# Raw weights and cached keys through four half-size buffers, and two more steps ahead of the sample gate product, in a one-core streaming encoder step

## The chip, the cores and the metric

The kernel runs on one core of a Trainium2 chip. The metric is device time in microseconds (us), the median of several runs; less is better. A profile is one more execution, recorded instruction by instruction. The engines are PE (matrix multiply), DVE (vector), ACT (scalar, activations and copies), POOL (GpSimd) and SP, which here does nothing but issue transfers (DMAs) one after the other.

## The reference, cut to what matters

One layer of an encoder runs on 1024 prompt rows and on 8 sample streams of 16 new rows with 1024 cached rows each. Three mixers share one input projection: a stick-breaking attention group (`sb`), a forgetting-attention group (`fox`) and a state-space group (`ssd`). Cross-attention and a feed-forward block follow.

```
proj = u @ w_in                                # w_in: 1024 x 3084
sq, sk, sv, fq, fk, fv, fg, z, xbc, dt = split_last(proj, IN_SIZES)
sb_o  = sb_attend(sq, [past sb_k, sk], [past sb_v, sv])
fcum  = cumsum([past fox_logf, log_sigmoid(fg + b)])      # gate sums over 1024 + 16 rows
fox_o = softmax(q.k/8 + fcum[q] - fcum[k]) @ v
ssd_o = rmsnorm(ssd_scan(conv(xbc), dt, ...) * silu(z))
h = h + [sb_o, fox_o, ssd_o] @ w_out ; h = h + cross_attend(h) ; h = h + swiglu(h)
```

The weights and the cached keys are float32. A dense product is made of three matmuls: each factor is split into a rounded high part and the remainder, and high*high, high*low and low*high are added up.

## The kernel before, in words

**Weights.** `raw_t` hands out a raw buffer `wr` of 128 x 1056 floats; there are two. `w_unit` loads a piece of a weight (512 KB: eight row blocks of 128 columns, four of 256 or two of 512) into one `wr` with one transfer (L306), and `split_unit` makes the high part `wh` of it by one ACT copy of 1024 columns (L289) and the low part `wl` by four POOL subtractions of 256 columns (L132). The matmuls are in `mm3` (L314, L315, L316). In the projection of the memory the raw weights go through other tiles (`st`).

**Cached keys.** A decode step handles two streams (p = 0 to 3, for `sb` and for `fox`). `load_k` fetches 512 keys of a stream into one `wr` (L850, 512 KB), PE transposes them (L856, eight 128 x 128 blocks), ACT copies them to `kf` (L857, twice 512 columns), and PE multiplies the queries with them (L844). A step makes four such loads: two halves of the rows for two streams. They take their `wr` from the same two buffers as the weights do.

**Gate sums.** `fox_sums` scans the log gates. For the sample streams it loads the cached gates (L669, 16-byte pieces), transposes them (L678), adds the new ones (L685), scans 32 rows of 1040 on DVE (L687), stores the result (L688), and forms `fnew` by a small matmul, the sample gate product: DVE forms its factor (L692), PE multiplies it with `hsel` (L696), DVE copies the product (L697).

**Order.** Generators give the order in which the work is written down. `pipeline` runs the attention rows (`prompt_rows` L547 to L550, decode rows) and the products with the values (L565 transposes, L580; for decode L887, L896) of `sb` and then `fox`: 72 row steps and 40 value steps, 112 in all. After each of its steps one step of `fill_all` is taken, and 1.1 steps per step once the dense part is over. The dense part, `fill_s`, has 66 steps: four projections of three, the values with nine, `fox_sums` with two, `z` with nine and nine, `dt` with one, and eight conv blocks of three. Behind it comes `ssd_gen` with 51 steps (L1017 prepare, L1032 weights, L1057 and L1063 states, L1117 outputs, L1129 write). What is left of it when the pipeline ends is woven into the output projection, `heads_out`, two of its steps per `ssd` step. By this count 50 of the 51 are done when the pipeline ends. A scheduler then sets the final order on each engine from this program, dependences and priorities, so that neighbours in the program may end up apart. Each engine runs its list strictly in order, and SP issues its transfers strictly in order too.

**Norm ahead of the feed-forward block.** `scaled` squares a row block of h on ACT (L1741, 1024 columns, into a `wr` that nobody reads) and takes the row sum from the accumulator.

Of the kernel before, what the change touches and what calls it, by code (L numbers as in the profile page):

```python
# [17 lines left out]
P = 128  # L18
D = 1024
# [38 lines left out]
def f32(x):  # L58
    return x.bitcast(F32)
# [3 lines left out]
def tile_hybrid_step(ctx: ExitStack, tc: tile.TileContext, a: dict):  # L63
    nc = tc.nc
    ACT, DVE, POOL, PE, SP = nc.scalar, nc.vector, nc.gpsimd, nc.tensor, nc.sync
# [13 lines left out]
    ring = over.enter_context(tc.tile_pool(name="ring", bufs=3, side="right"))  # L79
# [206 lines left out]
    def split_unit(raw, n, eng=POOL, pair=None):  # L286
        hi, lo = pair or (ring.tile([P, 1056], F32R, tag="wh", name="wh"),
                          ring.tile([P, 1056], F32R, tag="wl", name="wl"))
        ACT.copy(hi[:, :n], raw[:, :n])  # L289
        if eng is POOL:  # L290
            pool_tt(lo[:, :n], raw[:, :n], f32(hi[:, :n]), ALU.subtract)
        else:
            eng.tensor_tensor(out=lo[:, :n], in0=raw[:, :n], in1=f32(hi[:, :n]), op=ALU.subtract)
# [305 lines left out]
    def sg2_t(dt=F32):  # L599
        return ptp.tile([P, 256], dt, tag="so", name="so", bufs=4)  # L600
# [45 lines left out]
    def fox_sums():  # L646
# [7 lines left out]
        for hf in range(2):  # L654
            tp = pd()
# [5 lines left out]
        tp = pd()  # L661
        for b in range(8):
# [7 lines left out]
                     in_=a["cache_fox_logf"][0].rearrange("b k h -> (b k) h").rearrange("(u p) h -> p u h", p=P))  # L670
# [4 lines left out]
        for hf in range(2):  # L675
            tp = pd()
# [15 lines left out]
        DVE.tensor_tensor(out=y8[0:32, :P].rearrange("p (b t) -> p b t", t=DEC_S),  # L692
                          in0=sr[:, PAST:].unsqueeze(1).to_broadcast([32, 8, DEC_S]),
# [117 lines left out]
    def decode_units(m):  # L811
# [15 lines left out]
        def rows(p):  # L827
# [17 lines left out]
                                                moving(g // 2, g % 2), start=True, stop=True) for g in (3, 0, 1, 2)])  # L845

            def load_k(hf, b2):
                raw = raw_t()
                rv = raw[:, :1024].rearrange("p (k c) -> p k c", c=256)
                SP.dma_start(out=rv, in_=ck[2 * p + b2, hf * 512:(hf + 1) * 512, :]  # L850
                             .rearrange("(k p) c -> p k c", p=P))
                kf = ring.tile([P, 1056], F32, tag=("wh", "wl")[b2], name="kf")
                for nb in range(2):
                    tp = pT()
                    for k in range(4):
                        PE.transpose(tp[:, k * P:(k + 1) * P], rv[:, k, nb * P:(nb + 1) * P], ident)  # L856
                    ACT.copy(kf[:, nb * 512:(nb + 1) * 512], tp)  # L857
                return kf

            def emit_past(hf):  # L860
# [696 lines left out]
    q = []  # L1557
# [175 lines left out]
    def scaled(blk):  # L1733

        if blk in (1, 3, 5, 7, 8):
            xs = h[(blk - 1) // 2 * 2:blk + 1] if blk < 8 else h[8:]
            b0, n = blk + 1 - len(xs), len(xs)
            ss, scratch = small(n), raw_t()
            for i, x in enumerate(xs):
                SP.dma_start(out=h_sc[(b0 + i) * P:(b0 + i + 1) * P, :], in_=x)  # L1740
                ACT.activation(scratch[:, :D], x, AF.Square, accum_out=ss[:, i:i + 1])  # L1741
            r = rstd_of(ss, n, 1.0 / D)
            yield
            for i, x in enumerate(xs):
                DVE.tensor_scalar(x, x, r[:, i:i + 1], None, ALU.mult)
            yield
        if blk in (1, 3):
            for kps in ((0, 1), (2, 3)):
                u = transposed(blk - 1, 2, kps)
                yield  # L1750
                yield from right_factors(0, blk - 1, 2, kps, u)
        if blk == 5:
            for _ in range(4):
                ahead.append(next(now))
                yield
# [181 lines left out]
```

## Time and profile before

| | |
|---|---|
| Median of the runs | 1937.82 us (1937.67, 1937.82, 1940.25) |
| The profiled execution | 1935.64 us |
| Its span, from the first to the last instruction | 1933.8 us |
| PE busy / DVE / ACT / POOL | 1843.4 / 898.4 / 816.6 / 628.4 us |
| Mean granted clock of PE | 0.983 |

The profiled execution lies 1.84 us above its span and 2.2 us below the median of the runs. "Busy" is the time in which an engine's instructions run; behind an engine's idle time the profile puts what ended it ("<-DMA wr<-cache_sb_k" is a transfer into `wr`). The granted clock is the share of its full clock at which PE was allowed to run.

### The profile page before, as it was taken

What the parts mean: (1) busy time and instruction counts of PE and PEld (TensorE: products, weight loads), DVE (VectorE), ACT (ScalarE), POOL (GpSimd) and SP (SyncE); (2) the same over time, 40 slices, a digit from 0 to 9 for tenths busy, and PEclk for the clock granted to TensorE, in tenths of its full rate; (3) what the DMA queues carried; (4) which work ended last, traced back from release to release, by engine and by line L of the source; (5) the groups of instructions that cost most, each with busy time, mean ns of one, the idle gap of its engine ahead of it and who ended that gap; (6) DMA issues with size and microseconds to landing.
All of it is one profiled execution on the core that took longest, in us unless ns stands there. A gap on an engine that the chain in (4) does not pass through costs nothing.

```text
span 1933.8 us, 32139 instructions
## 1 busy us (share of the span) xinstructions
PE 1843.4 (95%) x12128; PEld 1646.3 (85%) x12128; DVE 898.4 (46%) x1802; ACT 816.6 (42%) x1702; POOL 628.4 (32%) x918
## 2 busy tenths in 40 slices
PE   7989997999898899999999999999999999999997
PEld 5889776898876677889998888999999999888886
DVE  3421324466646783354445378333333333455554
ACT  6431543444656772143333165333333333344443
POOL 6632415263424563211101213554544443000000
PEclk9999997999999989999999999999999999999999
DMA  9455646455487878435559123322233223557572
GB/s 335 139 163 152 205 124 171 131 147 163 139 256 244 259 236 299 153 124 164 164 166 342 59 95 97 95 69 69 72 78 89 71 69 90 193 195 237 176 241 90
DMA packets 328923, 307.52 MB, mean 159 GB/s; under 512 B 88637, under 2 KB 292517, under 8 KB 328769
## 3 DMA queue, kind: packets, MB, share of 16 engines
q1 hardware_dynamic: 328768, 305.48, 51.5%
q8 instruction: 95, 1.56, 0.3%
q14 instruction: 60, 0.48, 0.1%
HBM read 229.31 MB, written 76.11 MB: 158 GB/s over the span
## 4 chain that ended last, share of the span: by engine, by line
PE 79%; DMA 6%; DVE 4%; ACT 2%; POOL 1%; issue 1%; SPq 0%; ACTq 0%; POOLq 0%; DVEq 0%
PE psd L1804 11%; PE psd L314 9%; PE psd L316 9%; PE psd L315 9%; PE pst L1804 8%; PE pss L1804 4%; PE pss L314 3%; PE pss L315 3%; PE pss L316 3%; PE pso L1804 2%; PE pso L580 2%; PE pst L314 1%; PE pst L315 1%; PE pst L316 1%; PE pst L565 1%
## 5 line engine op out<-in xcount | busy, mean ns | idle before, releaser
L132 POOL TENSOR_TENSOR wl<-wr,wh 128x256 fp32r<-128x256 f32 (+1 forms) x180 | 134.2, 778 | 241.2 <-ACT wh L289 208.9
L314 PE MATMUL psd<-act,wh 128*128 128x384 f32 x576 | 198.5, 345 | 5.2 <-DVE sg L441 2.6
L316 PE MATMUL psd<-act,wl 128*128 128x384 f32 x576 | 197.5, 343 | 0.1
L315 PE MATMUL psd<-act,wh 128*128 128x384 f32 x576 | 197.2, 342 | 0.0
L1804 PE MATMUL pst<-bT,tr 128*128 128x256 f32 (+1 forms) x1068 | 155.0, 293 | 0.0
L1804 PEld LDWEIGHTS pst<-bT,tr 128*128 128x128 f32 x1068 | 144.9, 188 | 0.1
L314 PE MATMUL psd<-wh,act 128*128 128x256 f32 (+3 forms) x414 | 134.2, 327 | 3.9 <-DMA act<-osc 1.1
L316 PE MATMUL psd<-wh,act 128*128 128x512 f32 (+3 forms) x424 | 136.9, 324 | 0.0
L315 PE MATMUL psd<-wl,act 128*128 128x256 f32 (+3 forms) x414 | 133.6, 324 | 0.5 <-POOL wl L132 0.5
L1804 PE MATMUL psd<-bT,tr 128*128 128x320 f32 (+1 forms) x912 | 133.2, 295 | 1.0 <-DVE tr L1651 0.5
L251 POOL TENSOR_SCALAR sm<-sm 128x1 f32<-128x1 f32 (+2 forms) x30 | 9.2, 307 | 377.6 <-ACT y L1899 291.8
L1804 PEld LDWEIGHTS psd<-bT,tr 128*128 128x128 f32 x912 | 124.7, 188 | 1.9 <-DVE tr L1651 0.7
L314 PEld LDWEIGHTS psd<-act,wh 128*128 128x128 f32 x576 | 109.3, 190 | 9.3 <-DVE sg L441 3.4
L132 POOL TENSOR_TENSOR tr<-u,tr 128x256 fp32r<-128x256 f32 x110 | 82.9, 782 | 99.2 <-ACT tr L1647 81.7
L132 POOL TENSOR_TENSOR ws<-ws 128x256 f32<-128x256 f32 (+2 forms) x100 | 78.5, 813 | 112.2 <-DVE ws L507 84.5
L316 PEld LDWEIGHTS psd<-act,wl 128*128 128x128 f32 x576 | 109.1, 189 | 2.0 <-issue 1.3
L315 PEld LDWEIGHTS psd<-act,wh 128*128 128x128 f32 x576 | 109.3, 190 | 0.8 <-issue 0.6
L1779 DVE TENSOR_TENSOR tr<-tr,pst 128x256 f32<-128x256 f32 (+1 forms) x86 | 38.6, 449 | 137.5 <-ACT tr L1776 104.4
L132 POOL TENSOR_TENSOR tr<-raw,tr 128x256 fp32r<-128x256 f32 x94 | 69.4, 768 | 86.2 <-ACT tr L1647 77.8
L289 ACT CAST wh<-wr 128x1024 fp32r<-128x1024 f32 (+2 forms) x45 | 47.0, 1050 | 106.2 <-PE psd L316 42.6
L314 PEld LDWEIGHTS psd<-wh,act 128*128 128x128 f32 x414 | 79.5, 192 | 11.9 <-issue 1.7
L1647 ACT CAST tr<-tr 128x384 fp32r<-128x384 f32 (+1 forms) x70 | 37.7, 538 | 122.0 <-DMA tr<-hidsc 112.8
(597 smaller groups left out, 4709.1 us busy)
## 6 DMA issues: line engine op xcount, KB each, us to landing
u<-w_down SPq DMA_DIRECT2D x40, 512.0 KB
raw<-w_down SPq DMA_DIRECT2D x26, 512.0 KB
st<-qksc SPq DMA_DIRECT2D x48, 256.0 KB
wr<-w_in SPq DMA_DIRECT2D x22, 512.0 KB
tr<-hidsc SPq DMA_DIRECT2D x57, 192.0 KB
hidsc<-tr SPq DMA_DIRECT2D x34, 288.0 KB
qksc<-sg SPq DMA_DIRECT2D x48, 192.0 KB
wr<-cache_sb_k SPq DMA_DIRECT2D x16, 512.0 KB
```

The costliest lines, as they stand in the source:

```text
L132: POOL.tensor_tensor(out=out[:, a0:a1], in0=in0[:, a0:a1], in1=in1[:, a0:a1], op=op)
L251: POOL.tensor_scalar(v, ss, inv, EPS, ALU.mult, ALU.add)
L289: ACT.copy(hi[:, :n], raw[:, :n])
L314: PE.matmul(out, ah, bh, start=start, stop=False)
L315: PE.matmul(out, ah, bl, start=False, stop=False)
L316: PE.matmul(out, al, bh, start=False, stop=stop)
L565: PE.transpose(tp[:, o:o + P], w[:, (2 * kp + j) * P:(2 * kp + j + 1) * P], ident)
L580: return PE.matmul(po[r:r + 64, q_], vt[:, 2 * (k0 + i) + j, :], pfs[i][:, sl], start=start and k0 == 0 and (j == 0 or qp > 0), stop=k0 + ...
L1647: ACT.copy(hi, src)
L1779: DVE.tensor_tensor(out=at(out, g), in0=at(x, g), in1=ps[g][:, :GW[g]], op=op)
L1804: PE.matmul(dst[g][:, :GW[g]], x[:, ka], y[:, k, :], start=start and k == 0 and m == 0, stop=stop and k == 3 and m == 2, skip_group_check= ...
```

## The change

The two raw buffers become four of 528 columns. `w_unit` loads a piece as two halves with a transfer each (twice as many transfers, half the size, the same bytes and rows) and rounds each half by itself (two ACT copies of 512 columns in place of one of 1024; POOL's subtractions stay 256 wide). `load_k` loads 512 keys as two halves of 256 and transposes and copies half by half: 4 + 4 blocks, and each of its two ACT copies now writes two runs of 256 columns. The projection of the memory, which brings its own raw tiles, is as before. `scaled` squares two halves of 512 into two buffers, with an accumulator read each and one DVE addition (128 x 1 or 128 x 2). `fox_sums` gets two empty steps between the store of the scan and the sample gate product, so the dense part has 68 steps; by the count above 48 of the 51 `ssd` steps are then done when the pipeline ends, and three are woven into `heads_out`.

```diff
     def raw_t():
-        return ring.tile([P, 1056], F32, tag="wr", name="wr", bufs=2)
+        return ring.tile([P, 528], F32, tag="wr", name="wr", bufs=4)
...
     def w_unit(srcs, k0, nk, raw=None, pair=None, eng=POOL):
         n = sum(s[2] for s in srcs)
-        raw = raw_t() if raw is None else raw
-        rv = raw[:, :nk * n].rearrange("p (k n) -> p k n", n=n)
-        o = 0
-        for w, c0, cn in srcs:
-            SP.dma_start(out=rv[:, :, o:o + cn],
-                         in_=w[k0 * P:(k0 + nk) * P, c0:c0 + cn].rearrange("(k p) n -> p k n", p=P))
-            o += cn
-        hi, lo = split_unit(raw, nk * n, eng, pair)
+        raws = [raw_t(), raw_t()] if raw is None else [raw]
+        nk_ = nk // len(raws)
+        for i, r in enumerate(raws):
+            rv = r[:, :nk_ * n].rearrange("p (k n) -> p k n", n=n)
+            o = 0
+            for w, c0, cn in srcs:
+                r0 = (k0 + i * nk_) * P
+                SP.dma_start(out=rv[:, :, o:o + cn],
+                             in_=w[r0:r0 + nk_ * P, c0:c0 + cn].rearrange("(k p) n -> p k n", p=P))
+                o += cn
+        hi, lo = pair or unit_pair()
+        for i, r in enumerate(raws):
+            sl = slice(i * nk_ * n, (i + 1) * nk_ * n)
+            split_into(hi[:, sl], lo[:, sl], r[:, :nk_ * n], eng)
...
         for p in range(4):
             SP.dma_start(out=fqs[:, p:p + 1], in_=fs_sc[8 * p:8 * p + 8, 0, PAST:PAST + DEC_S])
+        yield
+        yield
         y8 = sg2_t()
...
             def load_k(hf, b2):
-                raw = raw_t()
-                rv = raw[:, :1024].rearrange("p (k c) -> p k c", c=256)
-                SP.dma_start(out=rv, in_=ck[2 * p + b2, hf * 512:(hf + 1) * 512, :]
-                             .rearrange("(k p) c -> p k c", p=P))
+                rvs = []
+                for q in range(2):
+                    rvs.append(raw_t()[:, :512].rearrange("p (k c) -> p k c", c=256))
+                    k0 = hf * 512 + q * 256
+                    SP.dma_start(out=rvs[q], in_=ck[2 * p + b2, k0:k0 + 256, :].rearrange("(k p) c -> p k c", p=P))
                 kf = ring.tile([P, 1056], F32, tag=("wh", "wl")[b2], name="kf")
-                for nb in range(2):
+                for q in range(2):
                     tp = pT()
-                    for k in range(4):
-                        PE.transpose(tp[:, k * P:(k + 1) * P], rv[:, k, nb * P:(nb + 1) * P], ident)
-                    ACT.copy(kf[:, nb * 512:(nb + 1) * 512], tp)
+                    for nb in range(2):
+                        for k in range(2):
+                            PE.transpose(tp[:, (2 * nb + k) * P:(2 * nb + k + 1) * P], rvs[q][:, k, nb * P:(nb + 1) * P],
+                                         ident)
+                    ACT.copy(kf[:, :1024].rearrange("p (n c) -> p n c", n=2)[:, :, q * 256:(q + 1) * 256],
+                             tp.rearrange("p (n c) -> p n c", n=2))
...
-            ss, scratch = small(n), raw_t()
+            ss, s2 = small(n), small(2 * n)
             for i, x in enumerate(xs):
                 SP.dma_start(out=h_sc[(b0 + i) * P:(b0 + i + 1) * P, :], in_=x)
-                ACT.activation(scratch[:, :D], x, AF.Square, accum_out=ss[:, i:i + 1])
+                for j in range(2):
+                    ACT.activation(raw_t()[:, :512], x[:, j * 512:(j + 1) * 512], AF.Square,
+                                   accum_out=s2[:, j * n + i:j * n + i + 1])
+            DVE.tensor_tensor(out=ss, in0=s2[:, 0:n], in1=s2[:, n:2 * n], op=ALU.add)
```

The scheduler's order changes with it on every engine, up to the cross-attention; behind that it is nearly the same. Three places matter below. In these rows the names are those of the tiles (`pss`, `psd`, `pst`, `pso` are banks of the result memory), and the changed file's line numbers are 12 to 18 higher at these lines.

The first is PE around the sample gate product (the row with `hsel`). Before:

```order
L685 MATMUL psd<-fold,so 32x16
L547 MATMUL pss<-st 128x128
L548 MATMUL pss<-st 128x128
L550 MATMUL pss<-mask_sb,identr 128x128
L547 MATMUL pss<-st 128x256
L548 MATMUL pss<-st 128x256
L550 MATMUL pss<-mask_sb,identr 128x128
L547 MATMUL pss<-st 128x384
L548 MATMUL pss<-st 128x384
L550 MATMUL pss<-mask_sb,identr 128x128
L696 MATMUL psd<-so,hsel 128x128
L756 MATMUL psd<-ident,xc 128x24 x8
```

And now, from the same small product (`fold`) on:

```order
L697 MATMUL psd<-fold,so 32x16
L559 MATMUL pss<-st 128x128
L560 MATMUL pss<-st 128x128
L562 MATMUL pss<-mask_sb,identr 128x128
L559 MATMUL pss<-st 128x256
L560 MATMUL pss<-st 128x256
L562 MATMUL pss<-mask_sb,identr 128x128
L559 MATMUL pss<-st 128x384
L560 MATMUL pss<-st 128x384
L562 MATMUL pss<-mask_sb,identr 128x128
L710 MATMUL psd<-so,hsel 128x128
L770 MATMUL psd<-ident,xc 128x24 x8
```

The same nine attention matmuls stand between the two products: the two empty steps moved nothing here, and one attention row more now follows behind the product.

The second is SP, where the cached gates for that scan are loaded (`cache_fox_logf`), with the last two key loads of a decode step ahead of it. Before:

```order
L475 DMA vsc_196<-so 128x256
L850 DMA wr<-cache_sb_k 128x4x256 x2
L669 DMA sg<-cache_fox_logf 128x64x4
L596 DMA mixsc<-sg 64x2x256
L306 DMA wr<-w_in 128x4x256
```

Now:

```order
L487 DMA vsc_196<-so 128x256
L866 DMA wr<-cache_sb_k 128x2x256 x3
L608 DMA mixsc<-sg 64x2x256
L866 DMA wr<-cache_sb_k 128x2x256
L681 DMA sg<-cache_fox_logf 128x64x4
L315 DMA wr<-w_in 128x2x256
```

The gate load has two transfers more ahead of it on the same queue, and a store (`mixsc`) that stood behind it.

The third is PE where the first `fox` rows meet the conv projection (the `mask_fx` rows). Before, a row's two pieces and the next row's first piece follow each other with only transposes between them:

```order
L731 MATMUL psd<-ident,so 27x128
L547 MATMUL pss<-st 128x512
L548 MATMUL pss<-st 128x512
L919 MATMUL pst<-fold_157,so 128x64
L565 MATMUL pst<-ident,ws 128x128 x8
L547 MATMUL pss<-st 128x128
L548 MATMUL pss<-st 128x128
L550 MATMUL pss<-mask_fx,identr 128x128
L547 MATMUL pss<-st 128x512
L548 MATMUL pss<-st 128x512
```

Now, from the conv block's tail transpose (`so`) at that place on:

```order
L745 MATMUL psd<-ident,so 27x128
L577 MATMUL pst<-ident,ws 128x128 x2
L562 MATMUL pss<-mask_fx,identr 128x128
L559 MATMUL pss<-st 128x512
L560 MATMUL pss<-st 128x512
L562 MATMUL pss<-mask_fx,identr 128x128
L577 MATMUL pst<-ident,ws 128x128 x3
L592 MATMUL pso<-pt,st 64x256 x4
L577 MATMUL pst<-ident,ws 128x128 x3
L326 MATMUL psd<-act,wh 128x384
```

Only one row of a single piece stands here now; the row ahead of it was begun 38 dense matmuls earlier, and the rows with two pieces come later, with dense matmuls between them.

More of the change, by code (lines that the diff above doesn't have):

```diff
@@ L284, in act_pair, with unit_pair, split_into, split_unit @@
                 lo[:, :KT * width].rearrange("p (k w) -> p k w", w=width))
[L286 to L289, printed above, removed]
+    def unit_pair():
+        return [ring.tile([P, 1056], F32R, tag=t, name=t) for t in ("wh", "wl")]
+    def split_into(hi, lo, raw, eng=POOL):
+        ACT.copy(hi, raw)
         if eng is POOL:
-            pool_tt(lo[:, :n], raw[:, :n], f32(hi[:, :n]), ALU.subtract)
+            pool_tt(lo, raw, f32(hi), ALU.subtract)
         else:
-            eng.tensor_tensor(out=lo[:, :n], in0=raw[:, :n], in1=f32(hi[:, :n]), op=ALU.subtract)
+            eng.tensor_tensor(out=lo, in0=raw, in1=f32(hi), op=ALU.subtract)
+    def split_unit(raw, n):
+        hi, lo = unit_pair()
+        split_into(hi[:, :n], lo[:, :n], raw[:, :n])
         return hi, lo
     def raw_t():
-        return ring.tile([P, 1056], F32, tag="wr", name="wr", bufs=2)
+        return ring.tile([P, 528], F32, tag="wr", name="wr", bufs=4)
     def w_unit(srcs, k0, nk, raw=None, pair=None, eng=POOL):
         n = sum(s[2] for s in srcs)
-        raw = raw_t() if raw is None else raw
-        rv = raw[:, :nk * n].rearrange("p (k n) -> p k n", n=n)
-        o = 0
-        for w, c0, cn in srcs:
-            SP.dma_start(out=rv[:, :, o:o + cn],
-                         in_=w[k0 * P:(k0 + nk) * P, c0:c0 + cn].rearrange("(k p) n -> p k n", p=P))
-            o += cn
-        hi, lo = split_unit(raw, nk * n, eng, pair)
+        raws = [raw_t(), raw_t()] if raw is None else [raw]
[12 more added lines that the diff above has]
+            split_into(hi[:, sl], lo[:, sl], r[:, :nk_ * n], eng)
         return (hi[:, :nk * n].rearrange("p (k n) -> p k n", n=n),
```

## The prediction

> **What bounds the kernel now.** I read the page first, then the busy time in stretches of 40 us, then what PE waited for, then the timeline at the longest waits.
>
> The page's span and its row of engines:
>
> ```profile
> span 1933.8 us, 32139 instructions
> PE 1843.4 (95%) x12128; PEld 1646.3 (85%) x12128; DVE 898.4 (46%) x1802; ACT 816.6 (42%) x1702; POOL 628.4 (32%) x918
> ```
>
> PE is the bound: it is idle for 90.4 us of 1933.8, and no other engine reaches half. So the change can win only a part of those 90 us, and time in which PE runs at a lower clock. The stretches tell where they lie (columns: stretch, length, busy time of PE, PE's weight load, DVE, ACT, POOL, then PE's granted clock, DMA share, GB/s):
>
> ```profile
> 280.00:320.00 40.00, 26.96 (x180) 21.21 (x178) 21.98 (x34) 19.93 (x45) 24.93 (x33) 0.79 0.87 184
> 480.00:520.00 40.00, 33.64 (x264) 31.07 (x263) 24.96 (x55) 21.90 (x43) 21.20 (x28) 0.96 0.47 136
> 560.00:600.00 40.00, 39.12 (x288) 27.68 (x286) 24.71 (x89) 27.47 (x61) 9.30 (x12) 0.96 0.61 192
> 600.00:640.00 40.00, 33.67 (x236) 25.77 (x234) 32.45 (x84) 27.50 (x62) 25.33 (x42) 0.96 0.89 263
> 640.00:680.00 40.00, 34.39 (x303) 26.43 (x299) 30.74 (x87) 29.81 (x66) 20.52 (x37) 0.96 0.88 277
> 680.00:720.00 40.00, 36.15 (x286) 29.65 (x283) 33.07 (x96) 29.43 (x69) 26.58 (x42) 0.87 0.71 218
> 720.00:760.00 40.00, 35.48 (x264) 26.92 (x263) 17.30 (x39) 15.14 (x30) 16.12 (x24) 0.96 1.01 355
> ```
>
> PE idles 13.0 us in 280 to 320, 6.4 in 480 to 520, and 0.9 + 6.3 + 5.6 + 3.9 + 4.5 = 21.2 us in 560 to 760, the `ssd` stage. PE's waits by what ended them (total, times, longest, in us):
>
> ```profile
> PE psd L696 <- DVE so L692: 6.3, 1, 6.3
> PE pss L547 <- DVE sm L521: 5.6, 4, 3.9
> PE pst L856 <- DMA wr<-cache_sb_k: 5.5, 4, 1.8
> PE pst L856 <- DMA wr<-cache_fox_k: 4.7, 4, 1.5
> PE pss L314 <- ACT wh L289: 1.8, 1, 1.8
> PE psd L314 <- ACT wh L289: 1.5, 2, 0.8
> ```
>
> So waits for keys in `wr` cost 10.2 us in eight places, waits for a rounded weight 3.3 us. These are what four smaller buffers can reach.
>
> **Keys in halves: a gain of 5.1 us.** The longest key wait, in the timeline (start, length, instruction, in brackets the idle time before it):
>
> ```profile
> 203.45 0.38 SPq L850 DMA_DIRECT2D wr<-cache_sb_k  x1
> 207.23 0.74 PE L856 MATMUL pst<-ident,wr 128*128 128x128 f32 x5 [1.82 <-DMA wr<-cache_sb_k]
> ```
>
> The load is issued only when the transposes have emptied its buffer, and PE has it 3.78 us later. With halves, the buffer's first half is free after four blocks instead of eight, its load starts about 0.5 us earlier (four transposes), moves half the bytes, and PE can start on it while the second half lands. No row shows a half key load. Bounds: from no gain (it lands no sooner; below nothing as well, see the rivals) to the whole 10.2 us. I take half, 5.1 us, because the transfer's moving part halves and its start does not. Nothing else is gained with these waits: each is under 2 us. ACT's two copies per load stay two; that each writes two runs costs nothing that I can see in a row, and I take zero, at most 0.1 us each where PE waits.
>
> **Weights rounded in halves: a gain of 1.3 us.** The rows of a whole ACT copy, of a pair of 512-column copies, of an issue and of the squares (the first, third, fourth and fifth row give minimum/median/maximum in ns):
>
> ```profile
> L289 ACT CAST wh<-wr x45: 1034/1048/1077, 64.8 to 1092.7; 128x1024 fp32r<-128x1024 f32 x41, 128x1040 fp32r<-128x1040 f32 x2, 128x1056 fp32r<-128x1056 f32 x2
> 280.35 1.05 ACT L857 COPY kf<-pst 128x512 f32<-128x512 f32 x2
> L850 SPq DMA_DIRECT2D wr<-cache_sb_k x16: 367/387/532, 167.7 to 455.8; - x16
> L1741 ACT ACTIVATE wr<-st x8: 1060/1062/1064, 1102.7 to 1141.5; 128x1024 f32<-128x1024 f32 x8
> L1741 ACT ACTIVATION_READ_ACCUMULATOR wr<-st x8: 182/185/192, 1103.7 to 1142.5; 128x1 f32 x8
> ```
>
> Two copies of 512 take 1.05 us back to back, as one of 1024 does, so 48 copies turned into 96 cost ACT nothing to speak of, and the first matmul can start after the first half, some 0.5 us sooner. Two waits are weight waits of this kind beyond the memory projection, which is not changed (1.8 and 0.8 = 2.6 us); half of them is 1.3 us, between 0 and 2.6. The Trainium skill, "ScalarE: Activation LUTs", section "What ACT_TABLE_LOAD costs", gives each instruction a fixed 186 ns, of which about 93 ns overlap back to back: an estimate from that page of 48 * 0.093 = 4.5 us more ACT work. The pair's row does not show it, and ACT is idle more than half of the time, so by either one the sum stays.
>
> The squares: nine of 1062 ns become eighteen halves, with nine more accumulator reads of 0.185 us and five small additions. Only the last row block's is not covered by dense matmuls: 0.19 plus about 0.15 us, a loss of 0.3 us.
>
> **The two empty steps: a gain of 0.9 us, and not where they stand.** The chain to the sample gate product, from the load of the gates to the dense matmuls behind it:
>
> ```profile
> 280.70 0.51 SPq L669 DMA_DIRECT2D sg<-cache_fox_logf  x1
> 281.31 6.57 SPq L596 DMA_DIRECT2D mixsc<-sg  x1
> 289.51 0.29 DVE L672 COPY sg<-sg 128x256 f32<-128x256 f32 x1 [4.16 <-DMA sg<-cache_fox_logf]
> 304.60 2.68 DVE L687 TENSOR_TENSOR_SCAN xc<-xc 32x1040 f32<-32x1040 f32 x1
> 308.99 0.73 DVE L692 TENSOR_TENSOR so<-xc,bmask 32x128 f32<-32x128 f32 x1
> 309.77 0.79 PE L696 MATMUL psd<-so,hsel 32*128 32x128 f32 x2 [6.27 <-DVE so L692]
> 311.91 0.42 PE L315 MATMUL psd<-wl,act 128*128 128x264 f32 x1
> 312.13 0.42 PE L316 MATMUL psd<-wh,act 128*128 128x264 f32 x1
> 317.43 0.28 PE L314 MATMUL psd<-wh,act 128*128 128x264 f32 x1
> 317.55 0.28 PE L315 MATMUL psd<-wl,act 128*128 128x264 f32 x1
> ```
>
> PE's order has the same nine matmuls between the small product ahead and this one, so I expect the 6.27 us to stay. What the steps do is to push two `ssd` steps out of the stage in which PE idles and under the dense output projection: 2 of 49 steps of a stage with 21.2 us idle, 0.9 us (from 0 to 2).
>
> The gate load itself is issued later: two more key transfers (0.39 us each) and a store (some 0.6 us) stand ahead of it, 1.4 us, less the 0.5 us by which the keys start sooner. DVE waited 4.16 us for it, and all that follows ends in an idle PE: a loss of 0.9 us (from 0 to 2).
>
> **The order at the first fox rows: a gain of 2.7 us.** PE after the 3.9 us wait:
>
> ```profile
> 504.02 0.50 PE L547 MATMUL pss<-st 128*128 128x512 f32 x1 [3.87 <-DVE sm L521]
> 505.26 0.52 PE L314 MATMUL psd<-act,wh 128*128 128x384 f32 x1
> 505.58 0.52 PE L315 MATMUL psd<-act,wh 128*128 128x384 f32 x1
> 508.59 0.33 PE L316 MATMUL psd<-act,wl 128*128 128x384 f32 x1
> 508.76 0.34 PE L314 MATMUL psd<-act,wh 128*128 128x384 f32 x1
> ```
>
> A row's bank was not free, because DVE was late. Behind the wait matmuls start every 0.32 us, later every 0.17, so from about 505 to 508 PE ran at half clock: some ten matmuls lose 0.15 us each, 1.5 us. The place costs 5.4 us. In the new order such rows are further apart, with 38 dense matmuls (38 * 0.17 = 6.5 us) of cover. The bounds are 0 and 5.4; I take half, since the scheduler can as well make such a wait elsewhere.
>
> **Sum.** 5.1 + 1.3 - 0.3 + 0.9 - 0.9 + 2.7 = 8.8 us off the profiled 1935.64, 1926.8; off the median of the runs, 2.2 us above that, 1937.8 - 8.8 = 1929.0. With the bounds this case reaches from about 1921 to 1936. About 0.2%, 3.9 us, is what a measurement of this kernel can tell from no change.
>
> **Rivals.** *The next thing is late (no difference).* Where keys come sooner, PE waits for the next link: ACT's copies to `kf`, or DVE, which is busy 30 of 40 us in the `ssd` stage. Then keys give 1 us, the fox rows nothing: 1.0 + 1.3 - 0.3 + 0.9 - 0.9 = 2.0 us, 1935.8. For it: the stage's DVE and ACT rows; against it: the trace puts those eight waits on the transfer.
>
> *A half takes as long as a whole (slower).* For it, in the chain of waits (start, length), a load of 256 KB and two of 512 KB:
>
> ```profile
> 123.44 4.33 DMA st<-qksc
> 203.45 3.64 DMA wr<-cache_sb_k
> 549.49 5.28 DMA wr<-cache_fox_k
> ```
>
> The small one was not shorter. If a load's time is mostly queue and landing, the second half, issued 0.39 us behind the first, lands later than the whole did: 8 * 0.39 = 3.1 us at the eight waits, 0.8 at two weights, 1.4 at the gate load, 0.3 at the squares, 5.6 us, and no gain: 1943.4. It decides if halves land less than 0.4 us sooner than wholes. Against it: that small load had company on the queue. The Trainium skill, "DMA: Bandwidth & Descriptors", section "Measured", asks for transfers of at least 1 MiB; a straight line through its 64 KB (0.95 us) and 1 MB (6.15 us) gives, as an estimate, 2.0 us for 256 KB and 3.4 for 512, so two halves cost 0.6 us more than a whole and 8 * 0.6 = 4.9 us at the waits. This trace, with no half key load, cannot confirm it.
>
> *The gate product's wait goes too (faster than forecast).* If DVE comes to the scan sooner, up to 6.3 us go, and 23 matmuls at 0.22 instead of 0.12 us behind it, 2.3 us: 1929.0 - 8.6 = 1920.4. The unmoved rows speak against it.
>
> **Chances.** Forecast 0.50, next thing late 0.18, half as long as a whole 0.18, gate product free 0.14. Faster 0.50 + 0.14 = 0.64, same 0.18, slower 0.18. The range, 1919 to 1941, holds the first, second and last and leaves out most of the third.
>
> **What would show it.** Right: waits of the transposes on `wr` fall from 10.2 to about 5 us; the product still waits 5 us or more; no wait of 3 us at the fox rows; PE idle falls by some 7 us. Wrong: PE idle unchanged with waits on `kf` copies or DVE in their place; half key loads that take over 3.4 us from issue; a new wait of several us in the stretch from 200 to 760, which the reordered engines may make anywhere.

## The result and the profile after

The changed kernel takes 1926.48 us (median of six runs, 1923.76 to 1928.87) beside 1940.38 us for the kernel before in the same comparison: a ratio of 0.9929, 95% interval 0.9912 to 0.9945, or 13.8 us less (10.7 to 17.1). The profiled execution took 1927.19 us, 8.45 less than that of before (1935.64). The changed kernel was timed in this one comparison; in the four later ones the kernel before had medians of 1934.70 to 1938.28 us, so the size of the gain is less sure than this interval says. Below, a difference in us is the ratio less one times the median of before in the same comparison.

The page's span and engines, after:

```profile
span 1925.5 us, 32425 instructions
PE 1837.7 (95%) x12128; PEld 1640.4 (85%) x12128; DVE 902.7 (47%) x1808; ACT 821.9 (43%) x1768; POOL 620.6 (32%) x922
```

PE executes the same 12128 matmuls, yet is busy for 5.7 us less (1843.4 to 1837.7); its idle time fell by only 2.6 us (90.4 to 87.8). A matmul lasts longer when the granted clock is low, so most of the gain in this profile is clock. Where it lies is told by three stages that hold the same matmuls in both kernels: up to the sample gate product, from there to the last output projection, and the rest. First before, then after (columns as in the prediction):

```profile
0.00:309.77 309.77, 271.25 (x1748) 239.69 (x1748) 101.07 (x185) 137.05 (x267) 137.02 (x204) 0.98 0.61 187
309.77:794.47 484.70, 450.10 (x3261) 378.46 (x3262) 275.74 (x652) 249.82 (x542) 200.57 (x309) 0.96 0.67 203
```

```profile
0.00:311.69 311.69, 273.35 (x1748) 241.55 (x1748) 101.75 (x186) 138.24 (x282) 137.61 (x207) 0.97 0.62 187
311.69:785.24 473.55, 442.58 (x3261) 371.18 (x3262) 279.35 (x650) 249.16 (x558) 195.94 (x313) 0.97 0.69 207
```

The first stage is 1.9 us longer, the second 11.1 us shorter: 7.5 of them busy time, 3.6 idle. The rest differs by 0.9. Some 40-us stretches of after:

```profile
280.00:320.00 40.00, 27.16 (x169) 20.25 (x169) 21.88 (x34) 21.53 (x51) 25.89 (x37) 0.79 0.91 186
400.00:440.00 40.00, 36.30 (x249) 32.21 (x242) 26.31 (x36) 16.65 (x41) 20.35 (x28) 0.91 0.41 111
480.00:520.00 40.00, 39.63 (x309) 36.96 (x308) 27.96 (x64) 27.25 (x59) 13.25 (x22) 1.00 0.59 169
680.00:720.00 40.00, 35.50 (x321) 27.31 (x320) 34.75 (x101) 32.79 (x76) 25.20 (x42) 1.00 0.86 291
```

480 to 520 is full and at full clock (33.64 busy and 0.96 before). 680 to 720 idles a little more than before (4.5 us, 3.9 before), but at clock 1.00 in place of 0.87: idle time that costs nothing more than itself. 280 to 320, where the gate product waits, is as bad as it was, and the loss in 400 to 440 is new. Before, that stretch was full:

```profile
400.00:440.00 40.00, 40.00 (x306) 37.26 (x306) 28.41 (x41) 18.24 (x42) 21.65 (x27) 1.00 0.42 118
```

PE's waits, after:

```profile
PE pso L914 <- DMA vr<-cache_sb_v: 5.7, 2, 4.2
PE psd L710 <- DVE so L706: 4.9, 1, 4.9
PE pst L872 <- DMA wr<-cache_fox_k: 4.5, 3, 2.4
PE pss L559 <- ACT ws L517: 4.5, 5, 1.7
PE pst L872 <- DMA wr<-cache_sb_k: 1.8, 3, 0.9
PE pss L559 <- DVE sm L533: 0.8, 2, 0.5
```

Waits for keys: 6.3 us in six places (10.2 in eight before). The wait for DVE at the rows: 0.8 (5.6). The product's: 4.9 (6.3). No wait for a rounded weight (`wh`) is left (3.3). In exchange the waits for the cached values (`vr`) rose from 3.5 to 5.7, and those of the rows for ACT from 0.8 to 4.5 us.

### The profile page after: what moved, and what is told of

Same layout as the page of the kernel before. It is cut to its first block, busy times and chain, and to the rows that moved or that the text cites. A ratio compares the mean times of both kernels' runs of the same rounds, so it can differ in the third digit from the quotient of the medians.

```text
span 1925.5 us, 32425 instructions
## 1 busy us (share of the span) xinstructions
PE 1837.7 (95%) x12128; PEld 1640.4 (85%) x12128; DVE 902.7 (47%) x1808; ACT 821.9 (43%) x1768; POOL 620.6 (32%) x922
## 4 chain that ended last, share of the span: by engine, by line
PE 79%; DMA 8%; DVE 4%; ACT 3%; POOL 3%; issue 2%; SPq 1%; ACTq 0%; POOLq 0%; DVEq 0%
PE psd L1825 11%; PE psd L326 10%; PE psd L327 10%; PE psd L328 10%; PE pst L1825 8%; PE pss L1825 4%; PE pss L326 3%; PE pss L327 3%; PE pss L328 3%; PE pso L1825 2%; PE pso L592 2%; PE pst L326 1%; PE pst L327 1%; PE pst L328 1%; PE pst L577 1%
## 5 line engine op out<-in xcount | busy, mean ns | idle before, releaser
L132 POOL TENSOR_TENSOR wl<-wr,wh 128x256 fp32r<-128x256 f32 (+2 forms) x184 | 139.5, 791 | 223.4 <-ACT wh L290 219.5
L132 POOL TENSOR_TENSOR ws<-ws 128x256 f32<-128x256 f32 (+2 forms) x100 | 73.3, 761 | 141.5 <-DVE ws L519 119.7
L290 ACT CAST wh<-wr 128x512 fp32r<-128x512 f32 (+2 forms) x90 | 52.4, 622 | 95.7 <-PE psd L328 31.1
```

Source lines behind the costliest of these rows:

```text
L290: ACT.copy(hi, raw)
```

## The experiments

Two theories were put against each other. The *halves* theory is the prediction's: keys and weights come sooner, the steps are worth 0.9 us. The *clock* theory says that the waits matter less by their length than by the half clock that some of them bring, and that the order of rows and dense matmuls, which the steps move, decides which do.

**The two steps alone**, in the kernel before:

```
+        yield
+        yield
         y8 = sg2_t()
```

> The kernel before with the two empty steps alone; buffers, loads, rounding and squares as before. The halves theory (the gain of 13.9 us is earned by keys and weights that come sooner) expects 1938 to 1941 us, 0.9 us of gain at most, the transposes' waits on wr still about 10 us, and the 3.9 us wait on DVE at the first fox rows still there. The clock theory (the gain is half-clock time of PE that went away since the order of the rows moved, 7.5 of the 8.3 us between the two profiles being PE busy time or waits that follow it) expects that moving ssd steps alone changes the half-clock time: a change of 3 us or more in either direction, and a PE busy time that moves with it by at least half of the change.

1930.10 us beside 1935.84: 0.9968 (0.9953 to 0.9982), 6.2 us less (3.5 to 9.1). The halves theory had at most 0.9 us for this, so as the whole story it falls. The clock theory's sign is not in this profile either: PE's busy time (1844.0 us) did not move with the time. (The profiled execution, 1932.85 us, is slower than the median and shows 2.8 of the 6.2 us.) The place of the product did move here: an attention row now stands ahead of it and takes its wait.

```profile
309.45 0.80 PE L547 MATMUL pss<-st 128*128 128x512 f32 x1 [6.04 <-ACT ws L505]
```

The waits on `wr` fell too, from 10.2 to 6.5 us, with loads and buffers as before; so a shorter wait for keys is by itself no sign that the halves made it.

**The halves alone**, the changed kernel without the two lines:

> The changed kernel without the two empty steps: halves of loads, rounding, keys and squares alone. The halves theory expects nearly all of the gain, 1927 to 1930 us, with waits of the transposes on wr of about 6 us as in the changed kernel. The clock theory expects the time to go where the half-clock time goes: if the half-clock spells between 500 and 785 us come back, 1934 to 1938 us, although the waits on wr are as short as in the changed kernel. If the two empty steps are what moved the order at the first fox rows, the wait of 3.9 us on DVE there is back.

1931.05 us beside 1935.84: 0.9967 (0.9951 to 0.9982), 6.4 us less (3.5 to 9.5). Each part brings about half, and 6.2 + 6.4 = 12.6 lies within the interval of the whole. Neither "nearly all" nor "the gain is gone" was right. The next rows show one place where the time with the halves is shorter. Before (start, length, instruction), then with the halves alone:

```profile
551.05 1.06 PE L844 MATMUL pss<-kf,act 128*32 128x512 f32 x8
...
554.90 0.63 PE L856 MATMUL pst<-ident,wr 128*128 128x128 f32 x4 [1.51 <-DMA wr<-cache_fox_k]
...
558.86 1.94 PE L844 MATMUL pss<-kf,act 128*32 128x512 f32 x8
...
564.42 0.60 PE L1017 MATMUL psd<-ident,act 128*128 128x128 f32 x4
```

```profile
547.40 1.06 PE L856 MATMUL pss<-kf,act 128*32 128x512 f32 x8
...
550.43 0.63 PE L870 MATMUL pst<-ident,wr 128*128 128x128 f32 x4
...
552.48 1.06 PE L856 MATMUL pss<-kf,act 128*32 128x512 f32 x8
...
556.23 0.60 PE L1033 MATMUL psd<-ident,act 128*128 128x128 f32 x4
```

The same matmuls take 13.4 us (551.05 to 564.42) and 8.8. The wait for keys was 1.51 us; the other 3 us are the half clock behind it, in which eight matmuls with keys take 1.94 us instead of 1.06. The 20 us around the place, with the granted clock in the third column from the end, before and with the halves:

```profile
548.00:568.00 20.00, 18.49 (x133) 13.78 (x133) 6.46 (x23) 10.70 (x26) 4.09 (x7) 0.83 1.08 328
```

```profile
544.00:564.00 20.00, 19.97 (x164) 16.04 (x162) 10.63 (x38) 15.01 (x38) 7.40 (x11) 1.00 1.04 322
```

The place does not belong to the halves alone: with the two steps alone the granted clock of 540 to 580 is 1.00 as well (0.91 before).

**Keys transposed as before, halves otherwise** (without the steps):

```diff
-                for q in range(2):
+                for nb in range(2):
                     tp = pT()
-                    for nb in range(2):
-                        for k in range(2):
+                    for k in range(4):
+                        PE.transpose(tp[:, k * P:(k + 1) * P], rvs[k // 2][:, k % 2, nb * P:(nb + 1) * P], ident)
...
+                    ACT.copy(kf[:, nb * 512:(nb + 1) * 512], tp)
```

> The changed kernel without the empty steps, and with the keys transposed in the order of before (four blocks of one column half, then four of the other), so that the first copy needs both half loads and neither half buffer is free before the second group: what is left is weights rounded in halves and four buffers. If the keys' halves bring the 6.4 us that the halves brought, this is within 2 us of the kernel before. If the weights' halves or the finer buffers bring it, it stays 4 to 8 us faster than the kernel before. PE's waits on wr are at about 10 us in the first case.

1935.90 us beside 1938.28: 0.9989 (0.9977 to 1.0001), 2.1 us less, within the first case. So about 4.3 of the halves' 6.4 us need the keys to be taken half by half; the two intervals (3.5 to 9.5 and -0.2 to 4.5) overlap, so this split is not sharp. The half clock is back at the same place:

```profile
550.00:570.00 20.00, 17.49 (x126) 12.89 (x125) 5.51 (x21) 9.70 (x23) 3.53 (x7) 0.83 1.02 313
```

Its waits on `wr`, and then those of the halves alone:

```profile
PE pst L869 <- DMA wr<-cache_fox_k: 3.2, 2, 2.5
...
PE pst L869 <- DMA wr<-cache_sb_k: 2.3, 4, 0.8
```

```profile
PE pst L870 <- DMA wr<-cache_sb_k: 2.3, 5, 0.6
```

They are 5.5 us, not 10: four buffers alone shorten them, but one of 2.5 us remains at the first fox keys, and with it the clock is lost. With the halves alone they are 2.3 us, none of them at fox keys.

**Keys by two transfers into one whole buffer**, in the kernel before: an early start without an early release.

```diff
-                SP.dma_start(out=rv, in_=ck[2 * p + b2, hf * 512:(hf + 1) * 512, :]
-                             .rearrange("(k p) c -> p k c", p=P))
+                for q in range(2):
+                    k0 = hf * 512 + q * 256
+                    SP.dma_start(out=rv[:, 2 * q:2 * q + 2, :],
+                                 in_=ck[2 * p + b2, k0:k0 + 256, :].rearrange("(k p) c -> p k c", p=P))
...
-                for nb in range(2):
+                for q in range(2):
```

> The kernel before (two buffers of 1056, weights whole) with the keys of each load brought by two transfers into the two halves of one buffer, transposed and copied half by half: an earlier start on the first half without an earlier release of the buffer. The halves theory expects part of the key gain, the waits on wr at 6 to 8 us instead of 10, and 1935 to 1939 us. The slower rival of the prediction (a half takes as long to land as a whole) expects the second half 0.4 us later than the whole was and 1941 to 1944 us. The clock theory expects the waits on wr to say little about the time, and the time to follow PE's half-clock time.

1944.24 us beside 1935.84: 1.0045 (1.0030 to 1.0060), 8.7 us *more*. This is the slower rival's size, but not its place: the waits on `wr` stayed at 10.2 us (in ten places), and the profile is longer in all three stages (by 2.2, 3.0 and 2.9 us), the last of which loads no keys. So an early start without the early release gained nothing here; what the 8.7 us are was not taken apart.

**Weights by two transfers into one whole buffer, rounded in halves**, in the kernel before:

```diff
...
+        for i in range(halves):
+            sl = slice(i * n // halves, (i + 1) * n // halves)
+            ACT.copy(hi[:, sl], raw[:, sl])
...
+        for i in range(halves):
...
+                SP.dma_start(out=rv[:, i * nk_:(i + 1) * nk_, o:o + cn],
```

> The kernel before (two buffers of 1056, keys whole) with each weight piece brought by two transfers into the two halves of one buffer and rounded half by half: earlier rounding without an earlier release. By the prediction's price it gains 1.3 us (0 to 2.6) and pays some issue time on SP: 1933 to 1937 us where the kernel before has 1936. If half transfers in one buffer only cost, as they did for the keys (8.5 us slower), it is slower by more than 3 us. If early rounding is the main part of what the halves brought, it is faster by 4 us or more.

1932.80 us beside 1938.28: 0.9971 (0.9959 to 0.9982), 5.6 us less. That is more than the 2.6 us that all weight waits were thought to hold, and their sum did not fall: 3.3 us in two places here, 1.8 + 1.5 = 3.3 before. The waits are not the same ones, though. Of the two that the prediction had named, that of 1.82 us is gone and that of 0.83 fell to 0.31; a new one stands elsewhere. Before, then in this run:

```profile
735.86 0.73 PE L314 MATMUL pss<-wh,ws 128*128 128x512 f32 x2 [1.82 <-ACT wh L289]
```

```profile
486.02 0.45 PE L320 MATMUL psd<-act,wh 128*128 128x384 f32 x1 [3.02 <-ACT wh L291]
```

So 2.3 us at the named places were gained and 3.0 lost at another, and the 5.6 us are not explained by them. In this profile, the fastest of the run's twelve executions, PE is busy for 4.7 us less than before and idle for 1.6 less; most of it is clock. The parts do not add up with the experiments above either: 5.6 less for weights here, 2.1 less with the same rounding in four buffers and keys transposed whole, 8.7 more for keys, 6.4 less for all. Each of these edits also moves the order (at 1233 of the 12128 places of PE's list another matmul stands here than before), so none of them is one thing.

**The two steps at the end of the dense part**, in the kernel before, so that two `ssd` steps are pushed on while z, dt and conv keep their places:

```diff
                 yield from xbc_proj(*o)
+        yield
+        yield
```

> The kernel before with the two empty steps at the end of the dense part, behind the last conv block, in place of ahead of the gate product: as many ssd steps (two) are pushed under the output projection, but z, dt and the conv blocks keep their places among the attention rows. If the steps gain by the two ssd steps that leave the stage with idle PE, this gains what the steps gained ahead of the gate product: 5.8 us, so about 1930 us where the kernel before has 1936. If they gain because the dense work behind the product moves two places later against the attention rows, this gains little: within 2 us of the kernel before.

1941.10 us beside 1938.28: 1.0009 (0.9990 to 1.0028). A gain of 0.9 us, as forecast for this reason, lies within the interval (1.9 less to 5.4 more); the 6.2 us of the steps do not. So pushed `ssd` steps are not what earns them.

**The two steps right behind the product**:

```diff
         DVE.tensor_copy(fnew, tp[:, :P])
         yield
+        yield
+        yield
```

> The kernel before with the two empty steps directly behind the sample gate product in place of ahead of it: all dense work behind the product (z, dt, conv) is two places later against the attention rows, as with the change, but the product keeps its place. If the steps gain by where the dense work falls against the rows, this gains about what the steps ahead of the product gained (4 to 8 us faster than the kernel before), and PE's waits for DVE at the rows (L547 <- DVE sm) fall to 2 us or less from 5.6. If they gain by the product's own place, this gains nothing (within 2 us) and the waits at the rows stay above 5 us.

1932.37 us beside 1936.37: 0.9980 (0.9964 to 0.9996), 3.9 us less (0.8 to 7.0), not to be told from the 6.2 ahead of it. What the two have in common is the place of the dense work behind the product against the rows, and, against what was expected, the row ahead of the product (6.23 us for ACT here). The waits of the rows for DVE, for steps ahead of the product, at the end, and behind it:

```profile
PE pss L547 <- DVE sm L521: 1.9, 2, 1.6
```

```profile
PE pss L547 <- DVE sm L521: 9.4, 7, 3.9
```

```profile
PE pss L547 <- DVE sm L521: 4.2, 7, 1.4
```

With the steps ahead of or behind the product, the wait of 3.9 us at the first fox rows is gone (4.2 in small pieces behind the product, not the 2 expected); at the end of the dense part it is there, as it is with the halves alone. This is the prediction's term "order at the first fox rows", and the steps bring it. It does not account for their gain. With the two steps alone, 480 to 520 idles 5.2 us less than before and at full clock, but 400 to 440 idles 3.0 us more, at 0.91, and 320 to 340 idles 3.6 us more, in a wait of 5.5 for the cached values (2.0 before):

```profile
480.00:520.00 40.00, 38.87 (x297) 36.17 (x297) 25.76 (x56) 24.13 (x48) 15.20 (x25) 1.00 0.57 168
400.00:440.00 40.00, 37.02 (x232) 34.13 (x225) 25.38 (x36) 16.90 (x39) 21.08 (x29) 0.91 0.33 98
```

These two places lose at least as much as the first gains. The loss in 400 to 440 of the changed kernel thus comes with the steps. Which places make up the 6.2 us stays open.

**Four steps ahead of the product**, in the kernel before:

> The kernel before with four empty steps ahead of the gate product in place of none (the change has two). If each pushed ssd step is worth as much as the two were, twice the gain: 10 to 12 us, about 1925 us. If the place of the dense work against the rows decides, there is no reason for twice the gain: anything from 4 us slower than before to 8 us faster, and PE's half-clock spells in other places again.

1943.27 us beside 1938.28: 1.0040 (1.0024 to 1.0057), 7.8 us more. The wait at the first fox rows is gone here too (480 to 520 is full, at clock 1.00), and the kernel is slower all the same. A pushed step has no price of its own; two happens to be a good number for this order.

**The gate load earlier**, in the changed kernel (in two halves that go to `fnew` and `pads`, which are free by then). It was planned for some 15 us earlier and is issued 26 us earlier, at 257.1 us in place of 283.0:

```diff
...
-        yield from proj_v(1, C_FV, p_v[1], s_v[1], extra=4)
+        for i, _ in enumerate(proj_v(1, C_FV, p_v[1], s_v[1], extra=4)):
+            if i == 2:
+                gate_load()
+            yield
```

> The changed kernel with the load of the cached gates issued about 15 us earlier on SP, into two small tiles that are free by then (two loads of 128 columns, two DVE copies in place of one, and two one-column POOL copies that hold the loads back until the third block of the values is done). If the sample gate product waits because the gate load comes late, its wait of 4.9 us and the half clock behind it (about 5 us in 296 to 320) shrink: 1919 to 1924 us. If it waits because DVE's scan stands behind other scans in its order, the wait stays and the time is within 3 us of 1926.5.

1929.84 us beside 1935.84: 0.9956 (0.9940 to 0.9973), so not better than the changed kernel's 0.9929. The product's wait fell from 4.9 to 2.8 us, and another grew from 3.4 to 7.1:

```profile
PE pst L912 <- POOL ws L132: 7.1, 2, 6.3
```

**The product behind the first z step, and behind the second**, in the changed kernel, so that 24 or 48 dense matmuls stand ahead of it:

```diff
...
+                for i, _ in enumerate(z_proj(int(o[1]))):
+                    if i == 0 and new_sums:
+                        new_sums.pop()()
+                    yield
```

> The changed kernel with the sample gate product written down one step later, behind the first z step, so that some 24 dense matmuls stand ahead of it on PE in place of three short rows. If the 4.9 us wait of the product and the half clock in 296 to 320 (5.4 us) are one stall that dense work can cover, 4 to 8 us are gained on the changed kernel: 1919 to 1923 us by its runs of 1926. If the dense matmuls' own operands are as late (the low parts wl from POOL, which was busy 26 of 40 us there), the wait moves to them, and the time is within 2 us of the changed kernel.

> As e10_defer0, with the product behind the second z step: some 50 dense matmuls ahead of it. Where the first one gains, this gains as much or up to 2 us more, since nothing reads the product's result before the decode rows of fox. If DVE's order is what makes the product late, the product is no longer waited for and the time lies with e10_defer0; if the moved order brings a wait of another kind, it is up to 4 us slower than e10_defer0.

1925.35 and 1925.47 us beside 1936.37: 0.9936 (0.9923 to 0.9950) and 0.9941 (0.9929 to 0.9953), no more than the changed kernel's gain. PE no longer waits for the product at all; it waits longer for the cached values instead (longest 6.6 and 7.8 us, 4.2 in the changed kernel). The wait and, from the chain of waits, the load that ends it (start, length), with the product behind one step:

```profile
PE pso L919 <- DMA vr<-cache_sb_v: 6.6, 1, 6.6
```

```profile
317.00 10.57 DMA vr<-cache_sb_v
```

In the changed kernel these value loads wait on SP, behind four small loads (L702) that need the store of the sums (L700) to have landed:

```profile
309.40 0.66 SPq L700 DMA_DIRECT2D fssc<-xc  x1
313.63 0.37 SPq L866 DMA_DIRECT2D wr<-cache_sb_k  x1
321.88 2.53 SPq L702 DMA_DIRECT2D fqs<-fssc  x4
...
326.12 1.00 SPq L923 DMA_DIRECT2D vr<-cache_sb_v  x2
```

**The store behind the value loads**, on top of the second of these (the four small loads move behind the `dt` step):

```diff
...
+        with tc.issue_after(last_v[0].ins):
+            SP.dma_start(out=fs_sc, in_=sr.unsqueeze(1).to_broadcast([32, DEC_S, PAST + DEC_S]))
```

> As e11_defer1, with the store of the scanned sums (L700, 512 rows of 1040 written from 32) put behind the value loads on SP, and the four small loads that read it back written down behind the dt step. If the 7.8 us wait for vr is made by that store (the value load landed in 10.6 us beside it in e10_defer0, in 4.7 without it), the loads land in 4 to 6 us, the wait falls below 3 us, and with the half clock behind it 4 to 8 us are gained on e11_defer1: 1918 to 1922 us where the kernel before has 1936. If the value loads are late since their buffers come free late, the wait stays above 5 us and the time is within 2 us of e11_defer1.

1922.11 us beside 1934.70: 0.9933 (0.9915 to 0.9951), the same as the changed kernel within the intervals. The load and the wait went as expected, from the chain and from the waits:

```profile
315.66 5.40 DMA vr<-cache_sb_v
```

```profile
321.11 1.93 PE L918 MATMUL pso<-vr,st 128*32 128x128 f32 x32 [2.14 <-DMA vr<-cache_sb_v]
```

So the load lands sooner ahead of the store (5.40 us) than behind it (10.57), and the longest wait fell from 7.8 to 2.14. The time does not show the 4 to 8 us. So no version here is shown to beat the changed kernel: the stage around the product has a row of late things, DVE, then POOL or the value loads, and in these runs taking one away uncovered the next.

## Why the prediction was right, point by point

*Direction and size.* Neither theory is the whole: the halves work in part through keys that are taken half by half and the clock that a key wait no longer costs, the steps by moving the order, in a way that stays open. Forecast 8.8 us off, 1929.0; measured 13.8 off (10.7 to 17.1), 1926.48, within the case's bounds (those of the terms, added up, give 1917.9 to 1940.1 and not "about 1921 to 1936"). The direction was right and the sum low, and that it came so near is in part luck. Its terms are idle time but for the half clock at the fox rows, and it expected PE to idle some 7 us less. PE idled 2.6 us less; the other 5.7 us of the profile's gain are clock. Two of its signs of being wrong appeared as well: half key loads over 3.4 us, and new waits of several us (4.2 for `vr`, the loss in 400 to 440).

*Keys in halves, 5.1 us.* About right. The waits on `wr` fell by 3.9 us with the whole change (10.2 to 6.3) and by 7.9 with the halves alone (to 2.3), and the experiment on the order of the transposes puts about 4.3 us on the keys. The waits alone would not show it, since with the steps alone they fell by 3.7. What the step left out is the half clock: 3 us of the 4.5 gained at 551 us are clock behind a wait of 1.5. The prediction gave half clock to two places (the rows and, in a rival, the product) and none to the keys.

*Weights in halves, 1.3 us.* The two waits it named are gone in the changed kernel, all 2.6 us and not half. What rounding in halves is worth in time stays open: 5.6 us by itself (3.5 to 7.9), 2.1 with four buffers (-0.2 to 4.5). The claim that the copies cost ACT nothing was wrong (and there were 45 of them by its own row, not 48):

```profile
L290 ACT CAST wh<-wr 128x512 fp32r<-128x512 f32 (+2 forms) x90 | 52.4, 622 | 95.7 <-PE psd L328 31.1
```

Ninety copies of 0.622 us take 56 us one by one and occupy 52.4, against 45 * 1.048 = 47 before: 5 us more. The Trainium skill, "ScalarE: Activation LUTs", section "What ACT_TABLE_LOAD costs", from which the prediction had an estimate of 4.5 us, agrees with this row. As argued, it cost no time that can be seen; ACT is busy 43%.

*The squares, 0.3 us of loss.* Not seen. PE is earlier than before by 8.6 us ahead of them (1085.20 against 1093.81 for the same matmul) and by 9.3 once they are through (1151.78 against 1161.04).

*The two steps, 0.9 us.* The reason is not shown: pushing two `ssd` steps gained nothing clear of noise by itself (1.7 us more, 1.9 less to 5.4 more), while steps at the product gained 6.2 (3.5 to 9.1). *The order at the first fox rows, 2.7 us.* The wait did fall, 5.6 to 0.8, with the half clock behind it; by the experiments it is the steps that do this. The two terms belong together and measured 6.2 where 3.6 were forecast. But 3.7 us of the rows' waits came back as waits for ACT (0.8 to 4.5), and the steps brought the loss in 400 to 440, which the sum did not have; so the two terms came near by other places than those they name.

*The gate load, 0.9 us of loss.* As forecast at its place: DVE waited 5.06 us for it, 0.9 more than 4.16, and the product came 1.9 us later.

```profile
291.12 0.29 DVE L684 COPY sg<-sg 128x256 f32<-128x256 f32 x1 [5.06 <-DMA sg<-cache_fox_logf]
```

*The product's wait stays.* It did (4.9, forecast 5 or more). "The two empty steps moved nothing here" holds for the changed kernel; with the steps alone a row moved ahead of the product. The rival in which it goes was tried by deferring the product: its wait went, and nothing was gained, since the value loads were next. That is the first rival, "the next thing is late", true at this place and not for the whole.

*"A half takes as long as a whole".* Its premise held at one of three places. From the chains, two half key loads of the changed kernel and one with the halves alone:

```profile
282.40 4.03 DMA wr<-cache_sb_k
...
593.64 8.72 DMA wr<-cache_fox_k
```

```profile
202.59 2.71 DMA wr<-cache_sb_k
```

The whole loads of the same keys, the first in the kernel before and the second with the two steps alone:

```profile
280.27 5.17 DMA wr<-cache_sb_k
...
602.77 8.24 DMA wr<-cache_fox_k
```

The whole load that answers to the third is the 3.64 at 203.45 us in the prediction. So two halves landed 0.9 and 1.1 us sooner than the whole, more than the 0.4 that decides for the rival, and one 0.5 later. The estimate of 2.0 us for 256 KB drawn from the Trainium skill ("DMA: Bandwidth & Descriptors", section "Measured") is below all three. The rival's conclusion did not follow. That the earlier release of the half buffer matters is argued from two runs: without it, two transfers into a whole buffer took 8.7 us more, and with keys transposed whole about 4.3 us of the gain were gone. No run has the release without the earlier start.

## What to carry to other kernels

Where PE is the bound and nearly full, count a wait with the clock behind it: a look at the granted clock in short stretches around each wait shows which waits cost twice or three times their length. What a load split in two brings is not told by the load alone: two transfers into one whole buffer cost 8.7 us for the keys here and gained 5.6 for the weights. And an edit that only moves steps changes which waits are covered: its price is neither proportional nor tied to one place, so try it alone, doubled and displaced, and add up the places that lose as well as the one that gains, before believing a reason for it.

## What the runs showed of the hardware

- A short wait can bring the half clock: the only wait in 548 to 568 us of the kernel before was 1.51 us long, and the clock there was 0.83. A wait of 1.82 us at 207 us left it full. In the fourteen profiles the granted clock is either 1.00 or 0.50, and its changes lie 3.41 us or a whole multiple of it apart. On that grid, each of the two waits falls whole into one stretch (first the stretch, then the next one):

```profile
552.69:556.10 3.41, 1.90 (x19) 1.84 (x19) 0.22 (x2) 1.06 (x2) 0.00 (x0) 1.00 1.11 330
556.10:559.51 3.41, 3.41 (x19) 2.63 (x21) 0.47 (x2) 2.16 (x7) 0.00 (x0) 0.50 1.08 318
```

```profile
204.55:207.96 3.41, 1.58 (x15) 0.76 (x8) 0.93 (x2) 2.68 (x8) 0.00 (x0) 1.00 0.86 232
207.96:211.37 3.41, 3.41 (x25) 3.41 (x23) 0.56 (x1) 1.60 (x3) 0.00 (x0) 1.00 0.99 322
```

  Counted over all fourteen profiles, without the first 20 and the last 6 us, a stretch at full clock in which PE idled 2.0 us or more was always followed by half clock (83 of 83), one with 1.2 to 2.0 us in 59 of 177 cases, one with 0.8 to 1.2 us in 2 of 171, one with less never (of 7125). So the idle time within one stretch, in one wait or several, tells most of it, and these two waits lie where it went either way; what decides there is open. The Trainium skill, "TensorE: Matmul & The Clock Gate", section "What's actually happening", has the clock fall after a whole idle window of about 3.4 us, in windows that run free of the kernel. The length of the window agrees with the grid; a whole idle one was not needed here.
- The same program varies with it: twelve runs with the steps behind the product took from 1923.27 us at a mean clock of 0.988 to 1939.46 at 0.982. One profile's clock is therefore one draw. In the profiles clock makes up 5.7 of 8.3 us of the gain; over the runs the mean clock rose from 0.9825 (the 85 runs of before in the experiments) to 0.985, and what share of the 13.8 us that is stays open.
- A 512 KB load beside a store of 2 MB in 512 rows, written from 32, took 10.57 us, and 5.40 with the store behind it; and on SP everything behind a load that needs it stood until it had landed (from 314.0 to 321.88 us in the changed kernel).
